# The residual sum of a two-model block kernel is kept in PSUM for the next norm, and ScalarE copies it back to SBUF

## The chip, the core and the metric

The kernel runs on one core of a Trainium2 chip. A core has five engines that run their own programs side by side and wait for one another by semaphores: TensorE (PE, the matmuls), VectorE (DVE), ScalarE (ACT), GpSimd (POOL) and SyncE (SP, which here issues most DMAs). The metric is the time of one execution on the device in microseconds (us), lower is better.

## The reference, cut to what matters

Two models run one after the other on 256 tokens of 1024 features. The first has two layers (gated delta rule and latent attention, each with a SwiGLU network) and a final norm; the second has two layers of four mixers in parallel and a gated network with a short convolution, its norms and residuals modulated by a condition. What the change touches are the residual sums and the norms:

```python
def first_block(x, ...):
    for i in range(DEPTH):                       # DEPTH = 2
        h = rms_norm(x, norm_mix[i])
        mix = gdn_mixer(h, ...) if i % 2 == 0 else mla_mixer(h, ...)
        x = x + mix
        x = x + swiglu(rms_norm(x, norm_ffn[i]), ...)
    return rms_norm(x, final_norm)

def second_block(x, c, ...):
    for l in range(DEPTH):
        sh1, sc1, g1, sh2, sc2, g2 = ...         # from the condition c
        h = rms_norm(x, norm1_g[l]) * (1.0 + sc1) + sh1
        y = ...                                  # four mixers on h @ w_in[l]
        x = x + g1 * (y @ w_out[l])
        h = rms_norm(x, norm2_g[l]) * (1.0 + sc2) + sh2
        x = x + g2 * conv_glu_ffn(h, ...)
    return x
```

All of it is float32. The kernel makes a float32 product out of three: each operand is split into a rounded part and the rest (h_hi and h_lo, wh and wl).

## The kernel before, in words

The work is eight stages in a row: g (gated delta rule), f0 (SwiGLU), a (attention), f1 (SwiGLU, then the final norm of the first model), m0 (mixers), f2 (gated network), m1, f3. x lives in SBUF as x_t, 128 partitions by two token tiles (t0, t1) of 1024 columns. Every stage ends with `proj_steps`: the projection runs into four PSUM accumulators ps_o, one for each token tile and half of 512 columns; the last weights are held back so that tile 0 is finished first and its norm can start while TensorE still works on tile 1. Between two stages lies what the text calls a seam, "f0 to a" and so on; there are seven.

At a seam, for each tile and half, VectorE adds x_t to the accumulator (L669; with a gate L671 and L672), ScalarE squares the sum and accumulates its mean (`stats`, L565), VectorE makes the reciprocal root in nine small operations (`rsqrt_1`, L527 to L534), multiplies it and the gain row into xn (`_norm`, L595), TensorE transposes xn into PSUM (ps_t, L605; in the stages of the second model L603 behind a matmul L598 that writes the shift), ScalarE casts that to h_hi (L608) and VectorE subtracts for h_lo (L609). The first matmul of the next stage (L492) needs h_hi, the second (L493) h_lo, the third (L494) h_hi with wl. Weights come by DMA into raw; ScalarE casts them to wh (L464), VectorE or GpSimd subtracts for wl (L469, L467). At f1 to m0 `final_norm` does two norms in one: the sum's Square (L689), a product with the gain (L690), its Square (L692), both roots at once (L694 to L521), and x_t written by VectorE (L704).

PSUM is split into two pools: `pa` with four buffers (ps_o, and later the accumulators of `first_units`) and `pm` with four or two, in which ps_t and the products of a stage live. The Squares' own output is thrown away (`junk`); it goes into ps_o itself.

The order of instructions on an engine is made when the kernel is built: a scheduler takes the work in written order, with the number `np` of a stage's plan lifting tile 0's norm (`high_priority`, L593), and puts each engine's instructions into one list. The engine takes them in that order, whatever is ready.

Of the kernel before, what the change touches and what calls it, by code (L numbers as in the profile page):

```python
# [25 lines left out]
NFF = 22  # L26
# [353 lines left out]
class Prog:  # L380
# [261 lines left out]
    def proj_steps(self, x, act, wap, nk, gate=None, order=None, each=None, last=None, out=None, hold=None):  # L642
        nc = self.nc
        tiles = lambda t: [a[:, k] for a in (t if isinstance(t, list) else [t]) for k in range(a.shape[1])]
        ps = [[self.pa.tile([128, 512], F32, name="ps_o", tag="acc") for _ in range(2)] for _ in range(2)]
        hold = hold or (self.more[2] if self.more else WSB)
        ch = {}
        for c in range(nk):
            o = order[c] if order else c
            ch[c] = self.weights(wap[o], CW, held=c >= nk - hold)  # L650
            if each:
                each(c)
            if c < nk - hold:
                todo = [(c, t, half) for t in range(2) for half in range(2)]
            elif c == nk - 1:
                todo = [(cc, t, half) for t in range(2) for half in range(2) for cc in range(nk - hold, nk)]
            else:
                todo = []
            ah, al = (tiles(t) for t in act)
            for cc, t, half in todo:  # L660
                k = order[cc] if order else cc
                self.mm3_b(ps[t][half], (ah[k][:, t * 128 : t * 128 + 128], al[k][:, t * 128 : t * 128 + 128]), ch[cc],
                           slice(half * 512, half * 512 + 512), cc == 0, cc == nk - 1)
            yield
        for t in range(2):
            for half in range(2):
                xs = x[:, t, half * 512 : half * 512 + 512]
                if gate is None:
                    nc.vector.tensor_tensor(xs, ps[t][half], xs, op=ALU.add)  # L669
                else:  # L670
                    nc.vector.tensor_tensor(ps[t][half], ps[t][half], gate[:, half * 512 : half * 512 + 512], op=ALU.mult)  # L671
                    nc.vector.tensor_tensor(xs, ps[t][half], xs, op=ALU.add)  # L672
                if out is not None:
                    nc.sync.dma_start(out[t][:, half * 512 : half * 512 + 512], xs)
            if last:
                last(t, ps[t])
            elif out is None:
                self.stats(x, t, ps[t])

    def final_norm(self, jp, pool, x, g, t, xg):  # L680

# [11 lines left out]
        v = pool.tile([128, 2], F32, name="fn_v", bufs=2)  # L693
        V.tensor_tensor(v, ss[:, :, 0], ss[:, :, 1], op=ALU.add)  # L694
        V.tensor_scalar(v[:, 0:1], v[:, 0:1], 1e-6, None, op0=ALU.add)
        V.scalar_tensor_tensor(v[:, 1:2], v[:, 0:1], 1e-6, v[:, 1:2], op0=ALU.mult, op1=ALU.add)
# [1575 lines left out]
```

## Time and profile before

| | us |
|---|---|
| three runs | 1572.02, 1565.72, 1570.32; median 1570.32 |
| profiled execution | 1570.74 |
| its span | 1569.0 |
| TensorE busy | 1455.1 (93%) |
| VectorE busy | 1120.2 (71%) |
| ScalarE busy | 811.7 (52%) |
| GpSimd busy | 659.3 (42%) |

The span is the time from the first to the last instruction of the profiled execution. Busy time is the time in which an engine has an instruction under way; TensorE's weight loads lie beside its matmuls. In a timeline each row has the start, the duration, the engine, the line, the operation, its tiles (out<-in), their shape, and in brackets how long the engine had been idle and what released it. PEclk is the granted clock of TensorE, 1.00 being 2.4 GHz.

### The profile page before, as it was taken

The page shows a single profiled execution, that of the slowest core. Times are in us where ns is not written, and L with a number is a line of the kernel's source. Part 1 is how long each engine was busy: PE and PEld are TensorE (multiplying, and loading weights), DVE is VectorE, ACT ScalarE, POOL GpSimd, SP SyncE. Part 2 cuts the span into 40 slices and gives each one's busy share as a digit, 9 for nine tenths or more (in the row PEclk, how much of TensorE's full clock was granted, in tenths as well). Part 3 has the DMA queues.
Part 4 walks back from the last instruction along what each step waited for, and adds up shares of the span by engine and source line. Part 5 has one row for each costly group of instructions (what it writes and reads, how often), then busy time and mean ns, then how long its engine had stood idle before and what let it go on. Part 6 is the DMA issues. An engine that isn't in the chain of part 4 may idle for free. (4 is left out here: it accounts for less than half of the span.)

```text
span 1569.0 us, 25783 instructions
## 1 busy us (share of the span) xinstructions
PE 1455.1 (93%) x9586; PEld 1286.3 (82%) x9586; DVE 1120.2 (71%) x2352; ACT 811.7 (52%) x1474; POOL 659.3 (42%) x433
## 2 busy tenths in 40 slices
PE   5999989899999899999988988998998899899998
PEld 4998878699988788999877766898987776589987
DVE  3588668778686577887477597788876768766752
ACT  4676545544543464554354665455544465466651
POOL 3577623256452522443136312465644622236530
PEclk9999999999999999999998999999999999999999
DMA  4756622677884455988434325576773442465551
GB/s 159 232 167 189 182 69 68 209 289 281 298 306 131 136 182 188 337 313 311 170 115 128 108 78 184 203 285 252 264 247 126 120 130 72 141 202 180 191 188 38
DMA packets 103246, 292.96 MB, mean 187 GB/s; under 512 B 28072, under 2 KB 37968, under 8 KB 96976
## 3 DMA queue, kind: packets, MB, share of 16 engines
q1 hardware_dynamic: 93872, 237.12, 44.9%
q10 hardware_dynamic: 8896, 53.14, 9.2%
q8 instruction: 75, 1.23, 0.3%
q0 software_dynamic: 352, 1.06, 0.2%
q14 instruction: 51, 0.42, 0.1%
HBM read 288.04 MB, written 3.24 MB: 186 GB/s over the span
## 5 line engine op out<-in xcount | busy, mean ns | idle before, releaser
L467 POOL TENSOR_TENSOR wl<-raw,wh 128x1024 fp32r<-128x1024 f32 (+4 forms) x162 | 405.6, 2511 | 414.6 <-ACT wh L464 350.7
L464 ACT CAST wh<-raw 128x1024 fp32r<-128x1024 f32 (+3 forms) x421 | 424.1, 1018 | 249.1 <-PE ps_o L493 97.4
L469 DVE TENSOR_TENSOR wl<-raw,wh 128x1024 fp32r<-128x1024 f32 (+2 forms) x259 | 356.9, 1385 | 145.2 <-ACT wh L464 143.2
L480 PE MATMUL ps_gu<-h_hi,wh 128*128 128x256 f32 x1280 | 313.1, 283 | 6.9 <-DVE gu_u L2226 6.3
L480 PE MATMUL ps_gu<-h_lo,wh 128*128 128x256 f32 x1280 | 312.7, 283 | 0.0
L480 PEld LDWEIGHTS ps_gu<-h_hi,wh 128*128 128x128 f32 x1280 | 244.9, 191 | 7.6 <-issue 6.7
L480 PEld LDWEIGHTS ps_gu<-h_lo,wh 128*128 128x128 f32 x1280 | 245.0, 191 | 0.1
L1394 DVE CUSTOM_DVE_ANT_0 ada_raw<-ada_raw,ada_cond 128x1024 f32<-128x1024 f32 x96 | 160.5, 1685 | 68.7 <-DMA ada_raw<-in_ada 68.7
L483 PE MATMUL ps_gu<-h_hi,wl 128*128 128x256 f32 x1280 | 179.2, 283 | 5.9 <-DVE wl L469 3.9
L483 PEld LDWEIGHTS ps_gu<-h_hi,wl 128*128 128x128 f32 x1280 | 164.4, 192 | 6.5 <-DVE wl L469 4.1
L494 PE MATMUL ps_o<-wl,act_h 128*128 128x512 f32 x352 | 138.8, 394 | 0.0
L493 PE MATMUL ps_o<-wh,act_l 128*128 128x512 f32 x352 | 138.6, 394 | 0.0
L492 PE MATMUL ps_o<-wh,act_h 128*128 128x512 f32 x352 | 138.3, 393 | 0.0
L2226 DVE SCALAR_TENSOR_TENSOR gu_u<-ps_gu,f2s,gu_u 128x254 f32<-128x254 f32 (+1 forms) x176 | 82.0, 477 | 40.7 <-ACT gu_u L2224 38.6
L738 POOL TENSOR_TENSOR act_l<-gu_t,act_h 128x256 fp32r<-128x256 f32 x44 | 51.8, 1179 | 102.7 <-ACT act_h L737 102.7
L2229 POOL TENSOR_TENSOR gu_t<-gu_t,gu_u 128x256 f32<-128x256 f32 x44 | 47.4, 1078 | 97.4 <-DVE gu_u L2226 84.1
L494 PEld LDWEIGHTS ps_o<-wl,act_h 128*128 128x128 f32 x352 | 66.1, 188 | 15.4 <-issue 0.5
L493 PEld LDWEIGHTS ps_o<-wh,act_l 128*128 128x128 f32 x352 | 66.1, 188 | 15.1 <-issue 0.2
L492 PEld LDWEIGHTS ps_o<-wh,act_h 128*128 128x128 f32 x352 | 66.1, 188 | 15.0 <-issue 0.2
L737 ACT CAST act_h<-gu_t 128x256 fp32r<-128x256 f32 x44 | 17.7, 407 | 95.8 <-DVE gu_t L736 95.8
L480 PE MATMUL ps_g<-h_hi,wh 128*128 128x256 f32 x256 | 66.5, 294 | 0.0
L480 PE MATMUL ps_g<-h_lo,wh 128*128 128x256 f32 x256 | 66.2, 293 | 0.0
(662 smaller groups left out, 2978.1 us busy)
## 6 DMA issues: line engine op xcount, KB each, us to landing
ada_raw<-in_ada ACTq DMA_DIRECT2D x48, 1024.0 KB, 6.2
raw<-in_f_gu SPq DMA_DIRECT2D x88, 512.0 KB, 5.4
raw<-in_u_gu SPq DMA_DIRECT2D x88, 512.0 KB, 4.2
raw<-in_f_dn SPq DMA_DIRECT2D x44, 512.0 KB, 6.2
raw<-in_u_dn SPq DMA_DIRECT2D x44, 512.0 KB, 4.3
raw<-in_g_qkv SPq DMA_DIRECT2D x32, 512.0 KB, 3.5
raw<-in_g_z SPq DMA_DIRECT2D x16, 512.0 KB, 5.7
raw<-in_g_out SPq DMA_DIRECT2D x16, 512.0 KB, 3.7
```

What stands on the lines that cost most here:

```text
L464: self.last_copy = nc.scalar.copy(wh[:, :cols], raw[:, :cols])
L467: nc.gpsimd.tensor_tensor(wl[:, :cols], raw[:, :cols], wh[:, :cols].bitcast(F32), op=ALU.subtract)
L469: nc.vector.tensor_tensor(wl[:, :cols], raw[:, :cols], wh[:, :cols].bitcast(F32), op=ALU.subtract)
L480: nc.tensor.matmul(ps, wh[:, k * width + m0 : k * width + m0 + m], xx[:, k, :], start=(n == 0), stop=(n == last))
L483: self.last_mm = nc.tensor.matmul(ps, wl[:, k * width + m0 : k * width + m0 + m], xh[:, k, :], start=False, stop=(n == last))
L492: nc.tensor.matmul(ps, xh, wh[:, sl], start=start, stop=False, **kw)
L493: nc.tensor.matmul(ps, xl, wh[:, sl], start=False, stop=False, **kw)
L494: nc.tensor.matmul(ps, xh, wl[:, sl], start=False, stop=stop, **kw)
L738: nc.gpsimd.tensor_tensor(al[:, m, :], t, ah[:, m, :].bitcast(F32), op=ALU.subtract)
L1394: nc.vector.tensor_tensor_reduce(raw[:, j], raw[:, j], self.cond, 1.0, 0.0, op0=ALU.mult, op1=ALU.add, accum_out=mod[:, i : i + 1])
L2226: nc.vector.scalar_tensor_tensor(u[:, j, d:], ps[:, j, : S - d], cw[:, 3 * q + 2 - d : 3 * q + 3 - d], u[:, j, d:], op0=ALU.mult, op1=ALU.add)
L2229: nc.gpsimd.tensor_tensor(t, t, u[:, 0], op=ALU.mult)
```

## The change

The sum is written into the accumulator ps_o in PSUM and not into x_t. The Square reads it there and throws its output away into a buffer of `pm`, the pool of the transposes. xn is made from ps_o, and ScalarE copies ps_o to x_t (L683 of the changed kernel). The last stage, whose sum is the output, is as before. `final_norm` works in PSUM in the same manner: the gain product is made in place, after the Square that reads the same half; the two roots are two chains of nine operations in place of one chain on two columns; x_t is written by ScalarE with the root as a scale (L707 in place of L704).

```diff
-    def stats(self, x, t, junk):
+    def stats(self, halves, t, junk):
...
-            nc.scalar.activation(junk[i], x[:, t, i * 512 : i * 512 + 512], AF.Square, scale=D**-0.5, accum_out=ss[:, i : i + 1])
+            nc.scalar.activation(junk[i], halves[i], AF.Square, scale=D**-0.5, accum_out=ss[:, i : i + 1])
...
         for t in range(2):
+            xs = [x[:, t, half * 512 : half * 512 + 512] for half in range(2)]
             for half in range(2):
-                xs = x[:, t, half * 512 : half * 512 + 512]
-                if gate is None:
-                    nc.vector.tensor_tensor(xs, ps[t][half], xs, op=ALU.add)
-                else:
-                    nc.vector.tensor_tensor(ps[t][half], ps[t][half], gate[:, half * 512 : half * 512 + 512], op=ALU.mult)
-                    nc.vector.tensor_tensor(xs, ps[t][half], xs, op=ALU.add)
+                p = ps[t][half]
+                if gate is not None:
+                    nc.vector.tensor_tensor(p, p, gate[:, half * 512 : half * 512 + 512], op=ALU.mult)
+                nc.vector.tensor_tensor(xs[half] if out is not None else p, p, xs[half], op=ALU.add)
...
             if last:
                 last(t, ps[t])
-            elif out is None:
-                self.stats(x, t, ps[t])
+            else:
+                self.stats(ps[t], t, [self.pm.tile([128, 512], F32, name="junk", tag="mm") for _ in range(2)])
+                self.scaled[t] = ps[t]
+                for half in range(2):
+                    nc.scalar.copy(xs[half], ps[t][half])
...
-    def final_norm(self, jp, pool, x, g, t, xg):
+    def final_norm(self, x, g, t, xg):
...
         for i, hv in enumerate(halves):
-            junk = jp.tile([128, 512], F32, name="fn_j", tag="gu_u", bufs=2)
-            nc.scalar.activation(junk, x[:, t, hv], AF.Square, scale=D**-0.5, accum_out=ss[:, 0, i : i + 1])
-            V.tensor_tensor(xg[i], x[:, t, hv], g[:, hv], op=ALU.mult)
-            junk = jp.tile([128, 512], F32, name="fn_j", tag="gu_u", bufs=2)
-            nc.scalar.activation(junk, xg[i], AF.Square, scale=D**-0.5, accum_out=ss[:, 1, i : i + 1])
+            for j in range(2):
+                junk = self.pm.tile([128, 512], F32, name="fn_j", tag="mm")
+                nc.scalar.activation(junk, xg[i], AF.Square, scale=D**-0.5, accum_out=ss[:, 2 * j + i : 2 * j + i + 1])
+                if j == 0:
+                    V.tensor_tensor(xg[i], xg[i], g[:, hv], op=ALU.mult)
...
-        self.rsqrt(rs, v, (128, 2), 1.0, 0.0, pool=pool, bufs=2)
+        self.rsqrt_1(rs[:, 1:2], v[:, 1:2], ss[:, 3:4], 0.0)
+        self.rsqrt_1(rs[:, 0:1], ss[:, 0:1], ss[:, 1:2], 1e-6)
         self.rstd[t] = rs[:, 1:2]
         self.scaled[t] = xg
-
-        def finish():
-            for hv in halves:
-                V.scalar_tensor_tensor(x[:, t, hv], x[:, t, hv], rs[:, 0:1], g[:, hv], op0=ALU.mult, op1=ALU.mult)
-
-        finish()
+        for i, hv in enumerate(halves):
+            nc.scalar.activation(x[:, t, hv], xg[i], AF.Copy, scale=rs[:, 0:1])
```

The change also moves instructions on the engines. Three places show how.

First, ScalarE at the seam f0 to a, before. The L565 rows are the Squares (tile 0's second, then tile 1's first, in one row of two, then tile 1's second), L608 is tile 0's cast to h_hi, L464 casts weights of stage a:

```order
L565 ACTIVATE ps_o,ss<-x_t 128x512 [waits DVE_49] x2
L608 CAST h_hi<-ps_t 128x4x128 [waits PE_49] x2
L464 CAST wh<-raw 128x704 [waits DMAHW4_49,Activation_49]
L464 CAST wh<-raw 128x704 [waits DMAHW5_49]
L565 ACTIVATE ps_o,ss<-x_t 128x512 [waits DVE_49]
L464 CAST wh<-raw 128x704 [waits DMAHW6_49,Activation_49]
```

The same place after, where L683 are the copies to x_t:

```order
L565 ACTIVATE junk,ss<-ps_o 128x512 [waits DVE_49]
L683 COPY x_t<-ps_o 128x512
L565 ACTIVATE junk,ss<-ps_o 128x512 [waits DVE_49]
L683 COPY x_t<-ps_o 128x512
L464 CAST wh<-raw 128x704 [waits DMAHW4_49,PE_49,Activation_49]
L464 CAST wh<-raw 128x704 [waits DMAHW5_49,PE_49]
L565 ACTIVATE junk,ss<-ps_o 128x512 [waits DVE_49]
L683 COPY x_t<-ps_o 128x512
L464 CAST wh<-raw 128x704 [waits DMAHW6_49,PE_49,Activation_49]
L608 CAST h_hi<-ps_t 128x4x128 [waits PE_49] x2
```

Before, tile 0's two casts came right behind tile 1's first Square. Now the copies, three weight casts and tile 1's second Square stand ahead of them.

Second, ScalarE at the seam f1 to m0, before, from tile 1's Squares on (w_sp is a weight of m0):

```order
L689 ACTIVATE fn_j,fn_ss<-x_t 128x512 [waits DVE_49,Activation_49]
L692 ACTIVATE fn_j,fn_ss<-ps_o 128x512 [waits DVE_49,Activation_49]
L689 ACTIVATE fn_j,fn_ss<-x_t 128x512 [waits DVE_49,Activation_49]
L692 ACTIVATE fn_j,fn_ss<-ps_o 128x512 [waits DVE_49,Activation_49]
L464 CAST w_sp<-raw 128x776 [waits DMAHW6_49]
L608 CAST h_hi<-ps_t 128x4x128 [waits PE_49] x2
```

After, where L695 are all the Squares, L707 the scaled copies to x_t (fn_r_8301 holds tile 0's roots, fn_r_8346 tile 1's), and L1911 is a small function of the mixers:

```order
L707 ACTIVATE x_t<-ps_o,fn_r_8301 128x512 [waits DVE_49]
L707 ACTIVATE x_t<-ps_o,fn_r_8301 128x512
L695 ACTIVATE fn_j,fn_ss<-ps_o 128x512 [waits DVE_49,Activation_49]
L464 CAST w_sp<-raw 128x776 [waits DMAHW6_49]
L695 ACTIVATE fn_j,fn_ss<-ps_o 128x512 [waits DVE_49]
L695 ACTIVATE fn_j,fn_ss<-ps_o 128x512 [waits Activation_49]
L695 ACTIVATE fn_j,fn_ss<-ps_o 128x512 [waits DVE_49]
L707 ACTIVATE x_t<-ps_o,fn_r_8346 128x512 [waits DVE_49]
L707 ACTIVATE x_t<-ps_o,fn_r_8346 128x512
L1911 ACT_TABLE_LOAD
L1911 ACTIVATE b_ls<-b_ls 128x2 [waits DVE_49]
L608 CAST h_hi<-ps_t 128x4x128 [waits PE_49] x2
```

Tile 0's casts now stand behind tile 1's copies, which need tile 1's roots, and behind a table load that came after them before.

Third, VectorE at the seam f2 to m1, before, from tile 0's products xn on (a_om to b_lpr are small preparations of the mixers):

```order
L595 SCALAR_TENSOR_TENSOR xn<-x_t,rstd,row 128x512 [waits DMASW2_49,DVE_49]
L595 SCALAR_TENSOR_TENSOR xn<-x_t,rstd,row 128x512
L672 TENSOR_TENSOR x_t<-ps_o,x_t 128x512 [waits DVE_49]
L1491 TENSOR_SCALAR a_om<-lay_12408 128x7 [waits DMAHW3_49]
L1493 TENSOR_SCALAR a_hw<-lay_12408 128x2
L1494 TENSOR_SCALAR a_hw<-lay_12408 128x2
L1496 TENSOR_SCALAR a_oka<-lay_12408 128x2
L1579 MEMSET a_cx 128x4
L1907 TENSOR_TENSOR b_lpr<-lay_12408 128x64 [waits DMAHW6_49]
L609 TENSOR_TENSOR h_lo<-ps_t,h_hi 128x4x128 [waits Activation_49]
L527 TENSOR_SCALAR rs_v<-ss 128x1 [waits Activation_49]
```

After, the end of tile 1's chain of small operations (L533, L534), tile 1's products xn, and h_lo:

```order
L533 TENSOR_SCALAR rs_t<-rs_h,rs_s 128x1 [waits DVE_49]
L1913 SCALAR_TENSOR_TENSOR b_nlam<-b_ls 128x1 [waits Activation_49]
L534 TENSOR_SCALAR rstd<-rs_t,rs_s 128x1 [waits DVE_49]
L595 SCALAR_TENSOR_TENSOR xn<-ps_o,rstd,row 128x512 [waits DVE_49]
L595 SCALAR_TENSOR_TENSOR xn<-ps_o,rstd,row 128x512
L609 TENSOR_TENSOR h_lo<-ps_t,h_hi 128x4x128 [waits Activation_49] x4
```

Tile 0's h_lo stood ahead of tile 1's chain (L527 begins it); now all four h_lo stand behind the chain and behind tile 1's xn.

## Rows read from the trace of the kernel before

**Rows 1.** The page: busy us, share, count per engine; one group of instructions

```profile
PE 1455.1 (93%) x9586; PEld 1286.3 (82%) x9586; DVE 1120.2 (71%) x2352; ACT 811.7 (52%) x1474; POOL 659.3 (42%) x433
...
L494 PE MATMUL ps_o<-wl,act_h 128*128 128x512 f32 x352 | 138.8, 394 | 0.0
```

**Rows 2.** Groups by line: count | busy us, mean ns | idle before, releaser

```profile
L605 PE MATMUL ps_t<-ident,xn 128*128 128x128 f32 x48 | 7.8, 293 | 8.4 <-DVE xn L595 8.4
L603 PE MATMUL ps_t<-ident,xn 128*128 128x128 f32 x128 | 17.0, 281 | 5.6 <-DVE xn L595 5.6
```

**Rows 3.** Groups by line, then line L595 with ns min/median/max

```profile
L565 ACT ACTIVATE ps_o<-x_t 128x512 f32<-128x512 f32 x24 | 14.5, 602 | 34.0 <-DVE x_t L672 19.3 <-DVE x_t L669 14.7
L627 ACT COPY first_raw<-ps_gt 128x512 f32<-128x512 f32 x8 | 4.7, 585 | 15.2 <-PE ps_gt L494 15.2
L671 DVE TENSOR_TENSOR ps_o<-ps_o,grow 128x512 f32<-128x512 f32 x16 | 11.2, 699 | 20.3 <-PE ps_o L494 20.3
...
L595 DVE SCALAR_TENSOR_TENSOR xn<-x_t,rstd,row x24: 740/748/2842, 302.6 to 1373.0; 128x512 f32<-128x512 f32 x24
L595 DVE SCALAR_TENSOR_TENSOR xn<-ps_o,fn_r,row x4: 741/744/744, 793.2 to 801.5; 128x512 f32<-128x512 f32 x4
```

**Rows 4.** Timeline, f0 to a: start us, us, instruction [idle before <-releaser]

```profile
498.29 1.26 ACT L608 CAST h_hi<-ps_t 128x512 fp32r<-128x512 f32 x2 [1.21 <-PE ps_t L605]
499.45 1.46 ACT L464 CAST wh<-raw 128x704 fp32r<-128x704 f32 x2
...
499.65 0.41 PE L493 MATMUL ps_ck<-wh,h_lo 128*128 128x320 f32 x1
506.84 0.63 PE L605 MATMUL ps_t<-ident,xn 128*128 128x128 f32 x4 [1.01 <-DVE xn L595]
```

**Rows 5.** Timeline, f1 to m0: TensorE and VectorE

```profile
793.97 2.05 PE L603 MATMUL ps_t<-ident,xn 128*128 128x128 f32 x16 [2.48 <-DVE xn L595]
796.53 0.45 PE L493 MATMUL ps_lk<-wh,h_lo 128*128 128x388 f32 x1 [0.28 <-DVE h_lo L609]
...
787.34 0.17 DVE L507 TENSOR_SCALAR rs_v<-fn_v 128x2 f32<-128x2 f32 x1
790.51 1.42 DVE L704 SCALAR_TENSOR_TENSOR x_t<-x_t,fn_r,fin_g 128x512 f32<-128x512 f32 x2
```

**Rows 6.** Timeline, f2 to m1: ScalarE, TensorE, VectorE

```profile
1187.42 1.28 ACT L1910 ACT_TABLE_LOAD   x1
...
1188.08 0.44 PE L493 MATMUL ps_lk<-wh,h_lo 128*128 128x388 f32 x1 [1.28 <-DVE h_lo L609]
...
1190.87 1.79 DVE L595 SCALAR_TENSOR_TENSOR xn<-x_t,rstd,row 128x512 f32<-128x512 f32 x2
```

**Rows 7.** Timeline, g to f0: ScalarE, TensorE, VectorE, GpSimd

```profile
304.19 1.19 ACT L608 CAST h_hi<-ps_t 128x512 fp32r<-128x512 f32 x2 [2.39 <-PE ps_t L605]
306.97 1.04 ACT L464 CAST wh<-raw 128x1024 fp32r<-128x1024 f32 x1 [0.98 <-DMA raw<-in_f_gu]
...
313.74 0.66 PE L605 MATMUL ps_t<-ident,xn 128*128 128x128 f32 x4 [1.45 <-DVE xn L595]
316.50 1.11 PE L605 MATMUL ps_t<-ident,xn 128*128 128x128 f32 x4 [2.11 <-DVE xn L595]
...
311.00 5.44 DVE L595 SCALAR_TENSOR_TENSOR xn<-x_t,rstd,row 128x512 f32<-128x512 f32 x2
...
310.31 5.59 POOL L467 TENSOR_TENSOR wl<-raw,wh 128x1024 fp32r<-128x1024 f32 x2 [12.80 <-ACT wh L464]
```

**Rows 8.** Timeline, a to f1: TensorE

```profile
605.66 1.32 PE L605 MATMUL ps_t<-ident,xn 128*128 128x128 f32 x8 [1.78 <-DVE xn L595]
```

**Rows 9.** Timeline, m0 to f2: ScalarE

```profile
971.38 1.04 ACT L464 CAST wh<-raw 128x1024 fp32r<-128x1024 f32 x1 [5.56 <-DMA raw<-in_u_gu]
```

**Rows 10.** Windows: us, busy (count) PE PEld DVE ACT POOL, PEclk, DMA, GB/s

```profile
788.00:796.00 8.00, 5.52 (x29) 3.90 (x27) 7.59 (x20) 4.14 (x10) 2.95 (x3) 1.00 0.02 10
1379.00:1386.00 7.00, 5.41 (x14) 4.01 (x15) 3.85 (x4) 2.51 (x4) 2.72 (x2) 0.57 0.73 239
```

More of the change, by code (lines that the diff above doesn't have):

```diff
@@ L665, in proj_steps @@
         for t in range(2):
+            xs = [x[:, t, half * 512 : half * 512 + 512] for half in range(2)]
             for half in range(2):
-                xs = x[:, t, half * 512 : half * 512 + 512]
-                if gate is None:
-                    nc.vector.tensor_tensor(xs, ps[t][half], xs, op=ALU.add)
-                else:
-                    nc.vector.tensor_tensor(ps[t][half], ps[t][half], gate[:, half * 512 : half * 512 + 512], op=ALU.mult)
-                    nc.vector.tensor_tensor(xs, ps[t][half], xs, op=ALU.add)
+                p = ps[t][half]
+                if gate is not None:
+                    nc.vector.tensor_tensor(p, p, gate[:, half * 512 : half * 512 + 512], op=ALU.mult)
+                nc.vector.tensor_tensor(xs[half] if out is not None else p, p, xs[half], op=ALU.add)
                 if out is not None:
-                    nc.sync.dma_start(out[t][:, half * 512 : half * 512 + 512], xs)
+                    nc.sync.dma_start(out[t][:, half * 512 : half * 512 + 512], xs[half])
+            if out is not None:
+                continue
             if last:
                 last(t, ps[t])
-            elif out is None:
-                self.stats(x, t, ps[t])
-    def final_norm(self, jp, pool, x, g, t, xg):
+            else:
[4 more added lines that the diff above has]
+    def final_norm(self, x, g, t, xg):
         nc = self.nc
@@ L685, in final_norm @@
         halves = [slice(i * 512, i * 512 + 512) for i in range(2)]
-        ss = pool.tile([128, 2, 2], F32, name="fn_ss", bufs=2)
+        ss = self.sm.tile([128, 4], F32, name="fn_ss", tag="fn_ss")
         for i, hv in enumerate(halves):
-            junk = jp.tile([128, 512], F32, name="fn_j", tag="gu_u", bufs=2)
-            nc.scalar.activation(junk, x[:, t, hv], AF.Square, scale=D**-0.5, accum_out=ss[:, 0, i : i + 1])
-            V.tensor_tensor(xg[i], x[:, t, hv], g[:, hv], op=ALU.mult)
-            junk = jp.tile([128, 512], F32, name="fn_j", tag="gu_u", bufs=2)
-            nc.scalar.activation(junk, xg[i], AF.Square, scale=D**-0.5, accum_out=ss[:, 1, i : i + 1])
[L693 to L696, printed above, removed]
+            for j in range(2):
[3 more added lines that the diff above has]
+                    V.tensor_tensor(xg[i], xg[i], g[:, hv], op=ALU.mult)
+        v = self.sm.tile([128, 2], F32, name="fn_v", tag="fn_v")
+        V.tensor_scalar(v[:, 0:1], ss[:, 0:1], ss[:, 1:2], 1e-6, op0=ALU.add, op1=ALU.add)
+        V.tensor_scalar(v[:, 1:2], v[:, 0:1], 1e-6, ss[:, 2:3], op0=ALU.mult, op1=ALU.add)
         rs = self.xp.tile([128, 2], F32, name=f"fn_r{t}")
-        self.rsqrt(rs, v, (128, 2), 1.0, 0.0, pool=pool, bufs=2)
+        self.rsqrt_1(rs[:, 1:2], v[:, 1:2], ss[:, 3:4], 0.0)
+        self.rsqrt_1(rs[:, 0:1], ss[:, 0:1], ss[:, 1:2], 1e-6)
         self.rstd[t] = rs[:, 1:2]
         self.scaled[t] = xg
-        def finish():
-            for hv in halves:
-                V.scalar_tensor_tensor(x[:, t, hv], x[:, t, hv], rs[:, 0:1], g[:, hv], op0=ALU.mult, op1=ALU.mult)
-        finish()
+        for i, hv in enumerate(halves):
+            nc.scalar.activation(x[:, t, hv], xg[i], AF.Copy, scale=rs[:, 0:1])
     def ffn1(self, x, i):
@@ L742, in ffn1 @@
                 nc.sync.dma_start(g, self.ap["fnorm"].partition_broadcast(128))
-            self.proj_out(x, (ah, al), self.ap[f"f_dn{i}"], NFF, each=self.ada_every(fp), last=(lambda t, junk: self.final_norm(fp, fin, x, g, t, junk)) if i else None)
+            self.proj_out(x, (ah, al), self.ap[f"f_dn{i}"], NFF, each=self.ada_every(fp), last=(lambda t, ps: self.final_norm(x, g, t, ps)) if i else None)
     def conv_silu(self, pool, dst, ps, mt):
@@ L761, in gdn @@
             for t in range(2):
-                self.stats(x, t, [self.pa.tile([128, 512], F32, name="junk", tag="acc") for _ in range(2)])
+                self.stats([x[:, t, i * 512 : i * 512 + 512] for i in range(2)], t, [self.pa.tile([128, 512], F32, name="junk", tag="acc") for _ in range(2)])
             self.prefetch(*((self.ap["g_z"][c], CW) for c in range(self.plan["pre"])))
```

## The prediction

> **What bounds the kernel now.** The page's busy shares come first: TensorE is busy 93% of the span, VectorE 71%, ScalarE 52% [rows 1]. The profiled execution took 1570.74 us (span 1569.0 and 1.7 around it); the median of the three runs is 1570.32, so the sum below is made against 1570.7 and needs no correction. Then the groups of instructions: the reader is to see that the projection's matmuls never sit idle (0.0 before 352 of them, [rows 1]), so that inside a stage nothing but TensorE's own work counts, and any delay at a seam between two stages is passed on in full. The third view is what TensorE waited for: the transposes of the norm waited 8.4 and 5.6 us for xn, 14.0 us over all seven seams [rows 2]. That is most of what a faster norm could give back. Everything else is a question of order at the seams, read in the timelines of four of them.
>
> **What is removed and added.** At six seams out of seven (and the final norm at the fourth) the sum now goes into PSUM. The same form, a VectorE product from PSUM and SBUF into PSUM, takes 0.70 us [rows 3], so the add itself changes by nothing that matters. The product xn reads PSUM: the four of that kind ran 0.741 to 0.744 us, the 24 from x_t 0.740 to 2.842, median 0.748 [rows 3]; alone no gain, beside GpSimd up to 2.1 us each. New on ScalarE are 24 copies from PSUM into x_t; the nearest row, the same shape, is 0.585 us (4.7 us over 8) [rows 3], 14 us in all on an engine that is half idle. The fourth seam loses four VectorE products, 1.42 us a pair [rows 5], and gains four ScalarE copies with a scale. No row shows that form; the plain copy (0.585) and the Square with its accumulation (0.60) [rows 3] bound it, and I take 0.6. VectorE's small operations there run 0.17 us [rows 5], 18 a tile for the two interleaved chains, about 3.1 us. As busy time all this is hidden. As order it is not.
>
> **The order is the cost.** ScalarE takes its instructions in program order. The order shown with the change has token tile 0's cast to h_hi behind tile 1's Squares and copies at every seam from g to f0 on, and VectorE's h_lo subtraction of tile 0 behind tile 1's chain at two. TensorE's first matmul of the next stage needs the h_hi cast and its second needs h_lo. Tile 0's transposes also wait for a Square of tile 1 now, because its throw-away output lies in the pool that the transposes write. Seam by seam, lateness of that second matmul (L493) after the change:
> - f0 to a. Before, ScalarE was free from 497.08 (498.29 less 1.21), cast at 498.29, and L493 ran at 499.65, 1.36 later [rows 4]. Now there stand in front of the cast a copy 0.59, two weight casts 1.46, a Square 0.60, a copy 0.59 and a weight cast 0.73: 3.97, so the cast is at 501.05 and L493 at 502.4, +2.8. The later gap of 1.01 [rows 4] may close (+1.7) or not, with tile 1's chain late too (+3.2). I take +2.5.
> - f1 to m0. TensorE's last projection matmul ends near 791.5 (793.97 less 2.48), and L493 runs at 796.53 [rows 5]. Now: add 0.7, Square 0.6, gain product 0.7, Square 0.6, chain 3.1, two scaled copies 1.2, a table load 1.28 that has moved ahead of the cast (its length [rows 6]), cast 0.59, h_lo 0.69 (no row, an estimate from the product of the same shape, 0.70). That is 9.5 and ends at 801.0, +4.5. The removed products (1.42) may let it start up to 1 us earlier; a weight product and small operations that VectorE has in between may add 1 to 2. +4 to +6.5; I take +5.4. Nothing is paid back, since TensorE had no other wait here.
> - f2 to m1. Tile 1's xn began at 1190.87; L493 of tile 0 ran at 1188.08, having waited 1.28 for h_lo [rows 6]. Now h_lo stands directly behind tile 1's two products: 1190.87 + 1.48 + 0.69 = 1193.0, +4.9; if tile 1's chain comes 0.5 to 1 earlier, +4. I take +4.7.
> - g to f0. The weight cast that waits for its DMA until 306.97 now stands ahead of tile 0's cast: 308.0 instead of 304.19 [rows 7], +3.8. In exchange the waits of 1.45 and 2.11 for tile 1's xn, which took 5.44 for two beside a GpSimd product [rows 7], go: -3.56. I take +0.5 (-0.5 to +2).
> - a to f1. In front of the cast: Square 0.6, copy 0.59, weight cast about 1.0 (1.46 for two narrower ones at f0 to a), so +2.2 to +3.2; the wait of 1.78 for xn [rows 8] goes: +0.4 to +1.4. I take +1.0.
> - m0 to f2. Tile 0's cast stood already behind a weight cast that waits 5.56 us for its DMA, to 971.38 [rows 9]; the four copies fit into that idle time. +0.5 (0 to +2); without that cover they would cost 2.4.
> - m1 to f3. Tile 0's shift matmuls, done before while xn was awaited, now wait for tile 1's Square. +0.5 (0 to +3).
> Sum: 2.5 + 5.4 + 4.7 + 0.5 + 1.0 + 0.5 + 0.5 = 15.1 us; with the low ends 9.6, with the high ends 23.
>
> One rule of the Trainium skill speaks against the change: "PSUM — Partial Sum Buffer", section on PSUM bank collisions, says that two engines must not access one bank at the same time, reads included. By it the Square, the copy and xn of one half, all from one bank, go one after another, where before xn read SBUF. At f1 to m0 that puts the two copies (1.2) ahead of xn, a wait that is in the sum already; without it the sum would be 13.9. No run here shows a collision.
>
> **The clock.** After the idle time at f1 to m0 (2.48 us) TensorE's clock stayed full, 1.00 from 788 to 796; at m1 to f3, after waits of 0.88 and 1.59, it was granted 0.57, mostly the 1.2 GHz level, from 1379 to 1386 [rows 10]. Such a stretch loses 7 x 0.43 = 3.0 us. With about 8 and 7 us of waiting at f1 to m0 and f2 to m1 none to two new ones are possible (0 to +6), and existing ones may vanish (to -2). I take +2. Forecast: 1570.7 + 15.1 + 2 = **1588 us**, its own range 1579 to 1596.
>
> **Rivals.** (a) *Faster, about 1562.* Mechanism: xn from PSUM no longer slows down beside GpSimd, at g to f0 (3.56) and a to f1 (1.78), and tile 1's norm comes earlier everywhere, so most of the 14.0 us of waits for xn go; about 9 would give 1562. For it: the four rows from PSUM within 0.003 us of one another. Against: the same order that brings tile 1 forward holds tile 0 back. It decides if the lateness of L493 at all seams together stays under what is paid back there, which needs tile 0's cast within about 1 us of its old time; the order excludes that at four seams. The Trainium skill, "SBUF — State Buffer", section on the two separate sides, says a VectorE operation with two SBUF inputs locks against GpSimd's reads, one port pair for both, and with one from PSUM it would not; the trace agrees (2.842 against 0.744). By that rule alone the time would be 1565.
> (b) *No change, about 1571.* Tile 1's matmuls, which need no norm chain any more when tile 0's are done, run without a gap, and TensorE takes up weights that have piled up meanwhile. For it: g to f0, where loss and gain nearly cancel. Against: a TensorE that has no idle time in the next stage cannot catch up.
> (c) *Slower still, about 1600.* Two or three new stretches at 1.2 GHz (3.0 each, +9 in place of +2) and the seams near their high ends (20).
>
> **How the numbers follow.** Forecast 0.60, (a) 0.10, (b) 0.17, (c) 0.13. Differences under 0.5% (7.9 us) can't be told from no change. Faster: (a), 0.10. Same: (b), 0.17. Slower: 0.73. The range 1567 to 1600 leaves out (a), the edge of (b) and half of (c).
>
> **What would show it.** In the changed profile L493 at f0 to a, f1 to m0 and f2 to m1 should come 2 to 6 us after its old distance from the last projection matmul, waiting for ScalarE's cast or VectorE's h_lo; xn should take 0.74 everywhere, and the waits before tile 1's transposes at g to f0 and a to f1 should be gone. TensorE's busy time should stay within 6 us of 1455. I am wrong if tile 0's casts come as early as before, if the 5 us at f1 to m0 or f2 to m1 are absent, or if the stages between the seams change by more than 5 us, since I cost the moved order there at nothing.

## The result and the profile after

The changed kernel takes 1582.44 us (median of 5 runs, 1578.18 to 1584.31), the kernel before 1569.74 beside it: 1.0097 times as long, 95% interval 1.0070 to 1.0124. That is 12.7 us slower; forecast were 1588 and slower. The profiled execution of after has a span of 1580.8, 11.8 more than before's 1569.0.

Cutting both profiles at the end of each stage's last projection matmul gives the length of a seam and the stage behind it. These are the three around the mixers in the profile after (m0, f2 and m1; windows: from and to, length, then busy time and count of TensorE, its weight loads, VectorE, ScalarE, GpSimd, the granted clock, DMA):

```profile
795.50:977.60 182.10, 158.60 (x915) 127.63 (x914) 125.67 (x478) 102.53 (x228) 72.66 (x64) 0.94 0.33 105
977.60:1191.10 213.50, 199.54 (x1323) 181.56 (x1323) 179.29 (x248) 110.98 (x179) 98.66 (x66) 0.99 0.72 255
1191.10:1378.00 186.90, 161.78 (x914) 129.27 (x913) 134.07 (x471) 99.50 (x220) 67.86 (x61) 0.94 0.33 105
```

The same cuts of five profiles, as lengths in us (e1, e3 and e5 are experiments below):

| stage with the seam before it | before | after | e3 | e1 | e5 |
|---|---|---|---|---|---|
| g (nothing changed in it) | 301.5 | 300.4 | 296.6 | 298.9 | 297.7 |
| g to f0, f0 | 197.7 | 199.0 | 196.0 | 192.8 | 198.9 |
| f0 to a, a | 97.3 | 99.8 | 97.7 | 97.2 | 98.2 |
| a to f1, f1 | 194.1 | 196.3 | 196.6 | 191.4 | 192.7 |
| f1 to m0, m0 | 172.6 | 182.1 | 182.2 | 170.3 | 174.7 |
| m0 to f2, f2 | 219.9 | 213.5 | 215.5 | 214.2 | 212.8 |
| f2 to m1, m1 | 180.0 | 186.9 | 188.1 | 181.9 | 182.8 |
| m1 to f3, f3 | 201.5 | 198.4 | 200.1 | 197.6 | 198.8 |

The reader is to see two things. The loss sits at the two seams into the mixers, 9.5 and 6.9 us. And stage g, which is the same program in all five, differs by up to 4.9 us from one execution to another, so a difference of 2 or 3 us in one stage of one profile proves nothing.

The page of after and TensorE's groups by line (count, busy us, mean ns, idle time before and its releaser), against [rows 1, 2]:

```profile
PE 1459.8 (92%) x9586; PEld 1291.4 (82%) x9586; DVE 1112.7 (70%) x2360; ACT 823.0 (52%) x1502; POOL 658.9 (42%) x433
...
L494 PE MATMUL ps_o<-wl,act_h 128*128 128x512 f32 x352 | 138.3, 393 | 0.0
L598 PE MATMUL ps_t<-ident,row 128*128 128x512 f32 x32 | 18.0, 662 | 3.7 <-ACT junk L565 3.2 <-ACT fn_j L695 0.5
L603 PE MATMUL ps_t<-ident,xn 128*128 128x128 f32 x128 | 16.7, 277 | 2.4 <-DVE xn L595 2.4
L605 PE MATMUL ps_t<-ident,xn 128*128 128x128 f32 x48 | 7.4, 301 | 4.5 <-ACT junk L565 4.5
```

The wait of the transposes for xn has fallen from 8.4 + 5.6 to 2.4 us, but 4.5 for `junk` and 3.7 for `junk` and `fn_j` have come in its place: 14.0 against 10.6 in all, so most of what the faster xn gave here is spent on a new wait.

The seam f0 to a after, ScalarE and then TensorE (start, duration, instruction, idle time before it and what released it); it answers to [rows 4]:

```profile
498.73 1.47 ACT L464 CAST wh<-raw 128x704 fp32r<-128x704 f32 x2
500.18 0.58 ACT L565 ACTIVATE junk<-ps_o 128x512 f32<-128x512 f32 x1
...
500.76 0.58 ACT L683 COPY x_t<-ps_o 128x512 f32<-128x512 f32 x1
501.23 0.79 ACT L464 CAST wh<-raw 128x704 fp32r<-128x704 f32 x1
501.91 1.08 ACT L608 CAST h_hi<-ps_t 128x512 fp32r<-128x512 f32 x2
...
502.56 0.42 PE L492 MATMUL ps_ck<-wh,h_hi 128*128 128x320 f32 x1 [2.28 <-ACT h_hi L608]
505.07 0.63 PE L493 MATMUL ps_ck<-wh,h_lo 128*128 128x320 f32 x1 [1.93 <-DVE h_lo L609]
```

The two weight casts, the Square, the copy and the third weight cast stand ahead of the cast to h_hi in just that order, and TensorE waits 2.28 us for h_hi and 1.93 for h_lo, where it had waited for neither.

f1 to m0 after, against [rows 5]:

```profile
802.54 1.26 ACT L707 ACTIVATE x_t<-ps_o,fn_r 128x512 f32<-128x512 f32 x2 [2.50 <-DVE fn_r L534]
803.82 1.28 ACT L1911 ACT_TABLE_LOAD   x1
805.12 0.20 ACT L1911 ACTIVATE b_ls<-b_ls 128x2 f32<-128x2 f32 x1
805.23 1.06 ACT L608 CAST h_hi<-ps_t 128x512 fp32r<-128x512 f32 x2
...
803.26 1.41 DVE L595 SCALAR_TENSOR_TENSOR xn<-ps_o,fn_r,row 128x512 f32<-128x512 f32 x2
...
805.85 0.69 PE L492 MATMUL ps_lk<-wh,h_hi 128*128 128x388 f32 x1 [5.79 <-ACT h_hi L608]
```

Tile 1's scaled copies, the table load and its function run first, then tile 0's casts; TensorE has stood still for 5.79 us. f2 to m1 after, TensorE and VectorE, against [rows 6]:

```profile
1196.99 0.45 PE L492 MATMUL ps_lk<-wh,h_hi 128*128 128x388 f32 x1 [1.54 <-ACT h_hi L608]
1200.66 0.69 PE L493 MATMUL ps_lk<-wh,h_lo 128*128 128x388 f32 x1 [3.22 <-DVE h_lo L609]
...
1198.60 1.41 DVE L595 SCALAR_TENSOR_TENSOR xn<-ps_o,rstd,row 128x512 f32<-128x512 f32 x2
1199.93 1.28 DVE L609 TENSOR_TENSOR h_lo<-ps_t,h_hi 128x512 fp32r<-128x512 f32 x2
```

h_lo comes right behind tile 1's xn, and the second matmul has waited 3.22 us for it. The waits for `junk`, of which the kernel before has none, stand at the three other seams (g to f0, a to f1 with the waits that follow it, m1 to f3):

```profile
303.29 1.97 PE L605 MATMUL ps_t<-ident,xn 128*128 128x128 f32 x8 [2.90 <-ACT junk L565]
...
600.80 1.09 PE L605 MATMUL ps_t<-ident,xn 128*128 128x128 f32 x8 [1.57 <-ACT junk L565]
602.71 0.56 PE L492 MATMUL ps_gt<-wh,h_hi 128*128 128x512 f32 x1 [0.81 <-ACT h_hi L608]
604.45 0.80 PE L493 MATMUL ps_gt<-wh,h_lo 128*128 128x512 f32 x1 [1.19 <-DVE h_lo L609]
...
1381.07 3.63 PE L598 MATMUL ps_t<-ident,row 128*128 128x512 f32 x4 [3.07 <-ACT junk L565]
```

The transposes, at m1 to f3 the shift matmul ahead of them (L598), wait 2.90, 1.57 and 3.07 us for the Square that writes `junk`, though they use nothing that it computes. It only holds the buffer. And xn from PSUM, as line L595 (ns: least, median, most) against [rows 3]:

```profile
L595 DVE SCALAR_TENSOR_TENSOR xn<-ps_o,rstd,row x24: 739/743/752, 300.4 to 1389.3; 128x512 f32<-128x512 f32 x24
L595 DVE SCALAR_TENSOR_TENSOR xn<-ps_o,fn_r,row x4: 742/748/752, 794.7 to 803.9; 128x512 f32<-128x512 f32 x4
```

All 28 take 0.739 to 0.752 us.

### The profile page after: what moved, and what is told of

Read it like the earlier page. It is cut to its first block, busy times and chain, and to the rows that moved or that the text cites. A ratio compares the mean times of both kernels' runs of the same rounds, so it can differ in the third digit from the quotient of the medians.

```text
span 1580.8 us, 25855 instructions
## 1 busy us (share of the span) xinstructions
PE 1459.8 (92%) x9586; PEld 1291.4 (82%) x9586; DVE 1112.7 (70%) x2360; ACT 823.0 (52%) x1502; POOL 658.9 (42%) x433
## 4 chain that ended last, share of the span: by engine, by line
PE 59%; DVE 14%; issue 4%; ACT 3%; DMA 2%; POOL 2%; ACTq 0%; DVEq 0%; POOLq 0%; SPq 0%
PE ps_gu L480 15%; PE ps_gu L483 8%; PE ps_o L493 6%; PE ps_o L492 6%; PE ps_o L494 6%; DVE wl L469 2%; DVE gu_u L2227 1%; PE ps_gt L493 1%; PE ps_gt L494 1%; PE ps_gt L492 1%; DVE ada_raw L1395 1%; ACT wh L464 1%; PE ps_u L480 1%; PE ps_bs L1976 1%; PE ps_t L603 1%
## 5 line engine op out<-in xcount | busy, mean ns | idle before, releaser
L467 POOL TENSOR_TENSOR wl<-raw,wh 128x1024 fp32r<-128x1024 f32 (+4 forms) x162 | 397.7, 2463 | 405.9 <-ACT wh L464 339.8
L464 ACT CAST wh<-raw 128x1024 fp32r<-128x1024 f32 (+3 forms) x421 | 423.3, 1019 | 237.6 <-PE ps_o L493 101.9
L469 DVE TENSOR_TENSOR wl<-raw,wh 128x1024 fp32r<-128x1024 f32 (+2 forms) x259 | 349.7, 1358 | 136.8 <-ACT wh L464 134.5
L1395 DVE CUSTOM_DVE_ANT_0 ada_raw<-ada_raw,ada_cond 128x1024 f32<-128x1024 f32 x96 | 172.2, 1807 | 53.7 <-DMA ada_raw<-in_ada 47.8
L492 PE MATMUL ps_o<-wh,act_h 128*128 128x512 f32 x352 | 138.4, 393 | 0.0
L493 PE MATMUL ps_o<-wh,act_l 128*128 128x512 f32 x352 | 138.3, 393 | 0.0
L2230 POOL TENSOR_TENSOR gu_t<-gu_t,gu_u 128x256 f32<-128x256 f32 x44 | 52.0, 1183 | 84.0 <-DVE gu_u L2227 78.0
L492 PEld LDWEIGHTS ps_o<-wh,act_h 128*128 128x128 f32 x352 | 66.1, 188 | 15.2
L493 PEld LDWEIGHTS ps_o<-wh,act_l 128*128 128x128 f32 x352 | 66.1, 188 | 15.0
L738 ACT CAST act_h<-gu_t 128x256 fp32r<-128x256 f32 x44 | 17.7, 406 | 101.1 <-DVE gu_t L737 101.1
L2231 ACT CAST act_h<-gu_t 128x256 fp32r<-128x256 f32 x44 | 17.9, 406 | 94.8 <-POOL gu_t L2230 94.8
```

The source lines that it names most:

```text
L464: self.last_copy = nc.scalar.copy(wh[:, :cols], raw[:, :cols])
L467: nc.gpsimd.tensor_tensor(wl[:, :cols], raw[:, :cols], wh[:, :cols].bitcast(F32), op=ALU.subtract)
L469: nc.vector.tensor_tensor(wl[:, :cols], raw[:, :cols], wh[:, :cols].bitcast(F32), op=ALU.subtract)
L492: nc.tensor.matmul(ps, xh, wh[:, sl], start=start, stop=False, **kw)
L493: nc.tensor.matmul(ps, xl, wh[:, sl], start=False, stop=False, **kw)
L1395: nc.vector.tensor_tensor_reduce(raw[:, j], raw[:, j], self.cond, 1.0, 0.0, op0=ALU.mult, op1=ALU.add, accum_out=mod[:, i : i + 1])
```

## The experiments

Two theories for the late casts were set against each other. Theory C is the prediction's: the new copies stand ahead of the casts on ScalarE. Theory J came from the waits for `junk`: the throw-away output of the Squares was moved from ps_o into the pool of the transposes, so tile 0's transposes must wait until tile 1's Squares have let go of it, and the scheduler, which knows this, sorts the casts behind everything that is ready earlier. Times are medians; ratios are to the kernel before, timed beside.

**e1: throw-away output in SBUF.** Everything else as changed.

```diff
-                self.stats(ps[t], t, [self.pm.tile([128, 512], F32, name="junk", tag="mm") for _ in range(2)])
+                self.stats(ps[t], t, [self.sm.tile([128, 512], F32, name="junk", tag="junk", bufs=1) for _ in range(2)])
...
-                junk = self.pm.tile([128, 512], F32, name="fn_j", tag="mm")
+                junk = self.sm.tile([128, 512], F32, name="fn_j", tag="junk", bufs=1)
```

> The changed kernel with one thing undone: the Squares' throw-away output goes to a buffer in SBUF, not into the pool of the transposes. Sum, xn and copies stay in PSUM and on ScalarE. Theory J (the throw-away buffers take the transposes' PSUM, so tile 0's transposes and casts are late): the cost at the seams goes, and the faster xn at g to f0 and a to f1 remains, so 1564 to 1572 us, with L493 at f0 to a within 1 us of its old distance. Theory C (the 28 new copies stand ahead of the casts, as the prediction put it): nothing changes, 1578 to 1586. Theory P (work in PSUM is itself slower): 1578 to 1586.

1555.52 against 1564.29 us, ratio 0.9947 (0.9929 to 0.9965): a little quicker than expected, and quicker than both kernels. Theory C and theory P fall: the copies are still in the program and the sum still in PSUM. At g to f0 (ScalarE, TensorE, VectorE, GpSimd):

```profile
299.49 1.18 ACT L608 CAST h_hi<-ps_t 128x512 fp32r<-128x512 f32 x2 [1.04 <-PE ps_t L605]
300.56 0.60 ACT L565 ACTIVATE junk<-ps_o 128x512 f32<-128x512 f32 x1
...
301.15 0.59 ACT L683 COPY x_t<-ps_o 128x512 f32<-128x512 f32 x1
...
307.29 1.31 PE L605 MATMUL ps_t<-ident,xn 128*128 128x128 f32 x8 [0.85 <-DVE xn L595]
...
306.48 1.41 DVE L595 SCALAR_TENSOR_TENSOR xn<-ps_o,rstd,row 128x512 f32<-128x512 f32 x2
...
305.97 4.93 POOL L467 TENSOR_TENSOR wl<-raw,wh 128x1024 fp32r<-128x1024 f32 x2 [11.72 <-ACT wh L464]
```

Tile 0's casts come ahead of tile 1's second Square again, with the copies still on ScalarE. Tile 1's two xn take 1.41 us together beside a GpSimd product, against 5.44 [rows 7], and TensorE waits 0.85 for them in place of 1.45 and 2.11. Over all seams the transposes' waits, the same groups as [rows 2], are down to 3.4 us from 14.0:

```profile
L603 PE MATMUL ps_t<-ident,xn 128*128 128x128 f32 x128 | 16.2, 277 | 2.5 <-DVE xn L595 2.5
L605 PE MATMUL ps_t<-ident,xn 128*128 128x128 f32 x48 | 7.4, 281 | 0.9 <-DVE xn L595 0.8
```

**e2: copies behind the casts.** The copies to x_t are written in the program after the casts of their tile; `junk` stays in the transposes' pool.

```diff
+                self.back[t] = [lambda half=half, xs=xs, t=t: nc.scalar.copy(xs[half], ps[t][half]) for half in range(2)]
-                for half in range(2):
-                    nc.scalar.copy(xs[half], ps[t][half])
...
                         nc.vector.tensor_tensor(ls, ps, hs.bitcast(F32), op=ALU.subtract)
+                for copy in self.back.pop(t, ()):
+                    copy()
                 yield
```

> The changed kernel with the copies to x_t written in the program behind the casts of their tile, nothing else. Theory J: the casts stay behind tile 1's Squares, since these still hold the transposes' buffers; 1578 to 1586, at most 3 us better by the copies that no longer stand ahead. Theory C: the casts come early again, 1566 to 1573.

1585.64 us, ratio 1.0137 (1.0115 to 1.0159), in the range of theory J. But the edit does not do what it was written for. Each copy, written behind xn, now waits for xn, and 18 of the 28 copies, all 14 of tile 0 among them, still run ahead of tile 0's casts. ScalarE at f0 to a (one line further down in this kernel: L685 is the copy, L566 the Square, L609 the cast):

```profile
496.00 0.59 ACT L685 COPY x_t<-ps_o 128x512 f32<-128x512 f32 x1 [0.52 <-DVE xn L596]
...
497.17 0.59 ACT L685 COPY x_t<-ps_o 128x512 f32<-128x512 f32 x1
497.64 0.60 ACT L566 ACTIVATE junk<-ps_o 128x512 f32<-128x512 f32 x1
...
498.91 1.08 ACT L609 CAST h_hi<-ps_t 128x512 fp32r<-128x512 f32 x2
```

Tile 0's two copies still stand ahead of its casts here, and only tile 1's first copy has gone; at f1 to m0 and f2 to m1 all four copies run ahead. So e2 does not decide between the theories. e1, with all copies, and e3, with none, do.

**e3: the kernel before with the one buffer moved.** No copies, the sum in SBUF, the old final norm.

```diff
-                self.stats(x, t, ps[t])
+                self.stats(x, t, [self.pm.tile([128, 512], F32, name="junk", tag="mm") for _ in range(2)])
...
-            junk = jp.tile([128, 512], F32, name="fn_j", tag="gu_u", bufs=2)
+            junk = self.pm.tile([128, 512], F32, name="fn_j", tag="mm")
```

> The kernel before with one thing of the change: the Squares' throw-away output goes into the transposes' pool. The sum is in SBUF, there are no copies, the final norm is the old one but for that buffer. Theory J: most of the loss without the rest of the change, and without the faster xn that pays some back, 1578 to 1590. Theory C: no copies, no loss, 1568 to 1572.

1582.48 us, ratio 1.0116 (1.0093 to 1.0140): where a buffer for values that nobody reads lies costs as much as the whole change. The stage table has the same two losses (m0 182.2, m1 188.1), and the same wait stands at g to f0, and at f0 to a the cast to h_hi is late too (TensorE, then ScalarE):

```profile
300.23 1.97 PE L605 MATMUL ps_t<-ident,xn 128*128 128x128 f32 x8 [3.61 <-ACT junk L565]
303.89 0.79 PE L493 MATMUL ps_gt<-wh,h_lo 128*128 128x512 f32 x1 [1.07 <-DVE h_lo L609]
...
494.70 1.06 ACT L608 CAST h_hi<-ps_t 128x512 fp32r<-128x512 f32 x2
```

**e4: both edits**, `junk` in SBUF and the copies written behind the casts.

> Both edits: throw-away output in SBUF and the copies behind the casts. Theory J: about as the first of these, 1562 to 1572, a little under it where one copy stood ahead of a cast. Theory C: 1566 to 1573, clearly under the first.

1559.49 us, ratio 0.9974 (0.9959 to 0.9989): in the range of theory J, but 4 us slower than e1, not a little quicker (the two intervals touch). Here too the copies wait for xn and run ahead of the casts or between them: at g to f0 the first cast starts 2.3 us after the last projection matmul, in e1 0.6. That this is the 4 us is not shown; that seam with its stage is as long as in e1 (192.9 against 192.8).

**e5: e1 with xn from SBUF**, to see what the rest of the change is worth.

```diff
-                self.scaled[t] = ps[t]
```

> The version with the throw-away output in SBUF, but xn is made from x_t in SBUF again (as ScalarE's copy has written it) outside the final norm. If the faster xn is what makes that version quicker than the kernel before, g to f0 and a to f1 lose 3.6 and 1.8 us of waits again, with a stretch at 1.2 GHz at g to f0 worth 3 to 5: 5 to 9 us slower than that version, ratio to the kernel before 0.998 to 1.002, and the longest xn over 2 us. If the source of xn does not matter (the gain is from tile 1's norm being ready earlier), the ratio stays at 0.993 to 0.997.

1565.93 against 1563.98 us, ratio 1.0012 (0.9995 to 1.0028): e1's whole gain is gone, some 10 us. At g to f0 (VectorE, GpSimd, TensorE):

```profile
305.29 5.35 DVE L595 SCALAR_TENSOR_TENSOR xn<-x_t,rstd,row 128x512 f32<-128x512 f32 x2
...
304.77 5.32 POOL L467 TENSOR_TENSOR wl<-raw,wh 128x1024 fp32r<-128x1024 f32 x2 [11.79 <-ACT wh L464]
...
307.94 0.66 PE L605 MATMUL ps_t<-ident,xn 128*128 128x128 f32 x4 [2.73 <-DVE xn L595]
310.69 1.12 PE L605 MATMUL ps_t<-ident,xn 128*128 128x128 f32 x4 [2.10 <-DVE xn L595]
```

The slow pair (5.35) and two waits like those of [rows 7] (2.73, 2.10) are there again, and behind them TensorE's clock is granted at 0.50 and 0.77, a good part of it at 1.2 GHz (windows; granted clock third from the end):

```profile
310.00:314.00 4.00, 3.31 (x12) 3.02 (x13) 1.93 (x3) 1.54 (x2) 0.09 (x1) 0.50 0.57 125
314.00:320.00 6.00, 6.00 (x22) 4.74 (x22) 0.00 (x0) 1.04 (x1) 0.00 (x0) 0.77 1.03 412
```

At the same seam of e1 it is full:

```profile
310.00:316.00 6.00, 6.00 (x33) 5.13 (x32) 0.00 (x0) 1.82 (x3) 0.90 (x1) 1.00 0.97 348
```

That is 4 x 0.50 + 6 x 0.23 = 3.4 us beside the 4.0 of longer waiting. So what PSUM is good for here is that xn reads it. That xn now comes after ScalarE's copy is not the loss: VectorE's xn waited for a copy once, 0.15 us, at f1 to m0.

How much of the 10 us is xn's own is less sure. xn is slow at three seams of e5, 5.35 us for two at g to f0, 3.28 at a to f1 and 1.79 at f2 to m1, and by the stage table these are 6.1, 1.3 and 0.9 us longer than in e1. Another 4.4 us lie in m0, where xn reads PSUM in both; its first 20 us are alike, and then e5's clock falls to 0.71 and 0.73 in two stretches of 10 us where e1's is at 0.95 or more. e9 below, whose edit lies in f2, took 174.2 us there, about as long as e5.

**e6: the changed kernel with the old final norm**, its sum in x_t and its `junk` in SBUF; the other seams as changed.

> The changed kernel with the old final norm (its sum in x_t, its Squares' output in SBUF, x_t written by VectorE); the six other seams as changed. Theory J: f1 to m0 is as before, so the 7 to 10 us lost from there to m0 go and the rest of the loss stays: ratio 1.002 to 1.006. If the final norm were innocent and the loss were spread evenly over the seams: 1.008.

1571.72 us, ratio 1.0052 (1.0030 to 1.0074), as theory J has it: about half of the loss belonged to f1 to m0 (its profile has m0 with that seam at 174.3 us).

**e7: e1 with the old final norm.**

> The version with the throw-away output in SBUF, with the old final norm. Tells what the final norm in PSUM with ScalarE's scaled copies is worth once the casts come early: that version's stage f1 to m0 was 2.2 us shorter than before, so ratio 0.995 to 0.997, within 3 us of it; if the old form is the better one, 0.992 to 0.994.

1557.98 us, ratio 0.9956 (0.9937 to 0.9974). It can't be told from e1: with `junk` in SBUF, the final norm in PSUM is worth nothing that these runs resolve.

**e8: the kernel before without GpSimd beside xn.** Two letters of stage f0's plan give two weight products to VectorE.

```diff
-        w='PPVVVPPVPVV...',
+        w='PPVVVVVVPVV...',
```

> The kernel before with two weight products of stage f0, the two that GpSimd ran beside tile 1's xn at g to f0, given to VectorE. If a GpSimd product beside it is what stretches xn from SBUF, the two xn there take 0.75 each in place of 5.44 together and the waits of 1.45 and 2.11 shrink to under 1.5 in all, though VectorE has 2.4 us more to do: 0 to 6 us quicker, ratio 0.996 to 1.000. If reading SBUF is slow by itself there, xn stays at 2 us or more and the ratio at 1.000 to 1.003.

1561.71 against 1564.80 us, ratio 0.9984 (0.9970 to 0.9999). VectorE and TensorE at g to f0:

```profile
311.05 1.41 DVE L595 SCALAR_TENSOR_TENSOR xn<-x_t,rstd,row 128x512 f32<-128x512 f32 x2
...
311.85 1.32 PE L605 MATMUL ps_t<-ident,xn 128*128 128x128 f32 x8 [0.52 <-DVE xn L595]
```

With nothing running on GpSimd there, xn from SBUF is as quick as xn from PSUM (1.41 for two), and the two waits shrink to 0.52. What stretched it at this seam was GpSimd's product, not SBUF. The Trainium skill, "SBUF — State Buffer", section on the two separate sides, has it that a VectorE operation with two SBUF inputs and a GpSimd operation that reads SBUF take turns on one pair of ports; e1, e5 and e8 agree (1.41, 5.35 and 1.41 us).

**e9: e1, and tile 0's norm lifted in stage f2** (its `np` from 0 to 60), so that at m0 to f2 the casts stand ahead of the weight cast that waits for its DMA.

> The version with the throw-away output in SBUF, and the number that lifts tile 0's norm in stage f2 from 0 to 60, so that at m0 to f2 tile 0's casts stand ahead of the weight cast that waits for its DMA, where they stood behind it in all kernels so far. If casts behind a waiting instruction are the cost at a seam, the wait for h_hi of 1 to 2 us at m0 to f2 goes: ratio 0.993 to 0.995. If not, no difference to that version (0.9947) beyond its interval.

1560.64 us, ratio 0.9976 (0.9957 to 0.9995): not better than e1. TensorE after the seam m0 to f2:

```profile
969.69 0.50 PE L492 MATMUL ps_gt<-wh,h_hi 128*128 128x512 f32 x1 [2.06 <-ACT h_hi L608]
```

The wait for tile 0's h_hi is gone, and one of 2.06 us for tile 1's has come in its place.

## Why the prediction was right, and where it was not

*Direction, size and order: right.* 12.7 us measured, 17.3 forecast, inside 1567 to 1600. The casts stood where the order had them. xn took 0.739 to 0.752 us everywhere, as forecast. The second matmul (L493), from the end of the last projection matmul, came later by 4.6 us at f2 to m1 (9.56 in place of 5.00; forecast 4.7), and at f1 to m0 the first (L492) by 5.2 (10.32 in place of 5.17), and the second as much (at 806.57; forecast 5.4).

*The cause: half wrong.* "The order is the cost" holds in so far as the late casts cost the time. But the step that priced it by what newly stands ahead of the casts, the copies among it, failed: e1 left the copies in and got everything back, e3 had none and lost all the same. At f0 to a, counted from the end of the last projection matmul, tile 0's casts start 0.9 us ahead of it in the kernel before and in e1, 2.5 behind it after, and 2.1 behind it in e3. The prediction named the right thing in one sentence, that tile 0's transposes wait for a Square "because its throw-away output lies in the pool that the transposes write", and gave it a term at m1 to f3 alone (+0.5). By e1 and e3 the casts were placed late because their input was late, and what stood ahead of them filled the time; how the scheduler came to its order was not looked at. The step left out was to ask why the order had changed.

*The seams of the sum.* By the stage table: f0 to a +2.5 (forecast 2.5), though L493 ran at 505.07 in place of 499.65, with the stage before it 0.2 later: 5.2 late instead of 2.8, of which half was paid back (from cast to L493 it took 3.2 us, not the 1.36 of the sum, since VectorE did small operations of stage a first, one of them 1.49 us, L1156); g to f0 +1.3 (0.5) and a to f1 +2.2 (1.0), the right kind, each a little more; f1 to m0 +9.5 (5.4 and a share of the clock); f2 to m1 +6.9 (4.7 and a share). m0 to f2 and m1 to f3 were forecast at +0.5 each and measured -6.4 and -3.1. Of neither is a cause shown; before's f2 of 219.9 us is the longest of all profiles, and e8, whose f2 is the same program, took 216.5, so a part is probably that one execution.

*The total: partly luck.* The other five seams with their stages cost 22.4 us where the sum had 14.1; m0 to f2 and m1 to f3 gave 9.5 back and stage g 1.1, which leaves the 11.8 between the two profiles. The prediction would have called itself wrong if a stage changed by more than 5 us, and m0 to f2 with f2 did (-6.4).

*One reading was off.* The sum at f1 to m0 starts at 791.5, taken as the end of the last projection matmul. In the trace that is the end of a shift matmul (L598); the projection ends at 790.64, and the chain as priced comes to +3.6 in place of +4.5. The measured 5.2 comes with VectorE's other work in the chain: from the last projection matmul to tile 1's roots 7.0 us passed after the change, where 5.7 were priced. The prediction's allowance of 1 to 2 us for such work covers the difference.

*The clock: 2 us forecast, of the right kind, and probably too little.* New waits are followed by stretches at the lower level, of which these are two (length, TensorE busy and so on, granted clock in the third column from the end):

```profile
604.00:611.00 7.00, 6.55 (x18) 5.17 (x19) 6.72 (x8) 2.92 (x4) 3.54 (x2) 0.58 0.52 176
805.00:812.00 7.00, 6.12 (x20) 5.72 (x21) 1.69 (x3) 1.27 (x4) 0.64 (x1) 0.55 0.00 0
```

Most of these 7 us ran at 1.2 GHz, at most 7 x 0.42 = 2.9 and 7 x 0.45 = 3.2 us lost, the second after the wait of 5.79, the first after waits of 1.57, 0.81 and 1.19. A shorter one follows the waits of 1.54 and 3.22 at f2 to m1 (0.57 from 1200 to 1204); at g to f0 the clock is as low as before (0.79 from 302 to 326 in both profiles). Others went: the stage table's windows have f2 at 0.99 against 0.96 before. TensorE's busy time rose by 4.7 us over all (1459.8 against 1455.1), at a mean granted clock of 0.971 against 0.972. But before's profiled execution is a low one: its other runs, timed beside the experiments, have 0.976 in the mean (0.972 to 0.983), after's five runs 0.970 to 0.972. A difference of 0.005 would be at most 0.005 x 1580 = 8 us (an estimate), so the clock may be a larger part of the loss than the sum had.

*Rival (a), faster.* Its mechanism was real. xn from PSUM is worth up to some 10 us (e5 against e1), and what kept it from deciding was just what the rival named, tile 0's casts in time. e1 gives them that and comes out at 0.9947.

*The PSUM rule* (the Trainium skill, "PSUM — Partial Sum Buffer", section on PSUM bank collisions). That a half's Square, copy and xn follow one another was priced at 1.2 us at f1 to m0. xn did begin, at 803.26, when the first of the two copies, 1.26 from 802.54, had ended, but VectorE was at small operations of the mixers until then (L1920), so the row shows no wait. The only waits of xn for a copy in any of the profiles are 0.2 us each, at this seam, in e5 and e9. And e7 shows that with `junk` in SBUF the whole of that final norm makes no difference that can be measured.

## What to carry to other kernels

Ask of a scratch buffer which pool it lies in and who else takes buffers there; an output that nobody reads can hold back the next stage through its buffer alone. When a built order has moved, look for the input that became late before pricing what now stands ahead. An operand moved to PSUM, so that VectorE no longer reads two operands from the memory that GpSimd is reading, is what made e1 quicker than the kernel before (0.9947 against e5's 1.0012). And when an experiment moves an instruction in the program, look in its trace whether the instruction moved: in e2 most copies had not.

## What the runs showed that was not expected

The Square costs the same wherever its output goes (0.58 to 0.60 us from PSUM into either memory), yet moving that output changed the time by 1.2% in one direction (e3) and by some 1.5% in the other (e1 against the changed kernel). TensorE's idle time is the span less its busy time (us; one profile each):

| profile | span | busy | idle | mean granted clock |
|---|---|---|---|---|
| before | 1569.0 | 1455.1 | 113.9 | 0.972 |
| after | 1580.8 | 1459.8 | 121.0 | 0.971 |
| e3 | 1577.2 | 1455.9 | 121.3 | 0.969 |
| e1 | 1548.7 | 1445.2 | 103.5 | 0.985 |
| e5 | 1561.0 | 1457.5 | 103.5 | 0.973 |

`junk` in the transposes' pool shows mostly as idle time (7.4 of 8.2 us from before to e3, 17.5 of 32.1 from e1 to after; e1's profiled execution, 1550.40, is near the quickest of its twelve). e5 is idle just as long as e1 in total, and its matmuls take 12.3 us longer at a lower mean clock, but that equality misleads: from g to f0 with f0 it is idle 3.9 us longer (5.1 against 1.3), and in stage g, the same program, 2.8 us shorter. Of the busy time, 2.2 us more are at g to f0 with f0, and 5.4 in m0, where xn is the same in both. Over all runs, not the profiles alone, the mean granted clock is 0.968 in e3, 0.971 after, 0.976 in e5 and in the kernel before, and 0.981 in e1; the slowest of these kernels is the one with the lowest clock, and the quickest the one with the highest.

`junk` alone costs 1.0116, the rest without it gives 0.9947, their product is 1.0062, and the whole change measured 1.0097. The intervals of these three are too wide to tell whether the two parts add.
